# A hybrid attention and state-space block on one core: table order, load queues and the pace of side work

## The chip, the cores and the metric

The kernel runs on one core of a Trainium2 chip. The metric is the device time of one execution in microseconds, as the median of several; the profile is of one execution.

## The reference

One layer of a streaming encoder, for 2048 new frames (the prompt) and 64 next frames of a running stream with 2048 cached frames (the sample). Cut to what matters here:

```
h = rms(x);  q, k, v, fg, u, hc, gb, gc = split(h @ w_in)       # 8 heads of 64; 16 state-space groups
c = cumsum(log_sigmoid(fg))
att = softmax(q k^T / 8 + c_q - c_k, causal) v                  # prompt: 2048 x 2048 per head
                                                                # sample: 64 x (2048 cached + 64)
h_t = A h_(t-1) + B u_t;  y = Re(C h_t) + d u                   # state space ("s5"), complex diagonal A
ssm = gelu(y) * sigmoid(gelu(y) @ w_glu + b_glu)
conv = gb * (three taps over gc * hc)
x = x + concat[rms(att), rms(ssm), rms(conv)] @ w_out
x = x + relu(rms(x) @ w_up)^2 @ w_down
```

All of it is float32, and the outputs are also the keys, values, gates and last states.

## The kernel before

The program has these stages: the projection (0 to 542.6 us in the profile), attention (542.6 to 1185.5), the output projection, the up and the down projection. Only the attention stage is touched.

**Products.** A float32 value is split into a high part `ph` (rounded to the format fp32r, for which TensorE has a quick product) and a low part `pl`, the difference. The probabilities times the values are three products: `ph` with both parts of `v` (L1260, L1262) and `pl` with the high one (L1267). Plain float32 products are used in the side work.

**Attention of the prompt.** Heads go one after the other. A head has four query blocks of 512 (`sb`), and for each the key tiles of 128 in pairs; that gives 24 units in a fixed list (`order()`). A unit does the scores of its tiles (two products, L1239 and L1240, `st`), the exponential on ScalarE (`p`, L1248), its rounding on ScalarE (`ph`, L1251) and the low part (`pl`, L1252) on VectorE or GpSimd. The products with `v` follow some units later (`pend`, `pend2`). Beside this, the row maxima of the next head are found: products `mx` (L1149) and VectorE's reductions `pm` (L1154). The tiles of a head are `kb`, `q1`, `ka` (2 MB together, loaded by `load(h + 1)` at a head's first unit), `v3`, and `q2` by query block (`load_q2`, three buffers), all loaded on SP's queue.

**Side work.** A chain of generators runs between the units. `s5_branch` makes tables on GpSimd and VectorE (`tables(q)`, four times: `z` and `e`, each a sum of two outer products with temporaries `tz` and `te`), then transposes and products on PE (`s5pg`, `s5pk`, `s5ps`), writes a kernel `kp_d` to memory, and loads it back in 8 shifted copies of 256 KB as a Toeplitz matrix (`s5mt`, L922). Then comes the recurrence over 16 steps of rows on GpSimd (L931 to L935), and the attention of the sample (`sample_attention`, for the pairs of heads 0 and 1, then 2 and 3); at last the outputs `s5py`, the gated unit `s5pz` (L1020), the loads of `w_out` and `out_sample`.

**What sets the order.** `fill(w)` is called in each unit with the unit's weight `w` (2.2 for a pair of full tiles, 1.2 on the diagonal; 40.8 in a head). It moves a clock on by 1.68 `w` and adds `w` to a budget (at most 4). While the budget is positive and the clock has come to the time that the chain asked for, the chain takes its next step; a step that yields a number above 0 costs 0.4 and is not gone on with before that much clock has passed, one that yields 0 costs 1.25. So each engine's list of instructions is fixed when the program is built; nothing is decided on the chip.

```
def fill(w):
    clock.now += w * 1.68
    clock.budget = min(clock.budget + w, 4.0)
    while clock.budget > 0 and clock.now >= clock.ready:
        y = next(it, None)
        ...
        clock.ready = max(clock.now + y, clock.ready)
        clock.budget -= 0.4 if y > 0 else 1.25
```

Of the kernel before, what the change touches and what calls it, by code (L numbers as in the profile page):

```python
# [13 lines left out]
ALU = mybir.AluOpType  # L14
# [34 lines left out]
def f32(ap):  # L49
    return ap.bitcast(F32)  # L50
# [735 lines left out]
def s5_branch(g, pool, sp):  # L786

    nc, I, O = g.nc, g.I, g.O
# [62 lines left out]
    po.memset(kp[:, :, 0:112], 0.0)  # L851

    def tables(q):
        z = zts[q % 2]
        gs = slice(4 * q, 4 * q + 4)
        sh = [128, 4, 16, 16]
        tz = tt[:, :1024].rearrange("p (g s c) -> p g s c", g=4, s=16)
        for dst, a, b in ((z, u1, bbr), (tz, u2, bbi)):
            g.tc.keep_in_program_order(po.tensor_tensor(
                dst, a.rearrange("p s g -> p g s")[:, gs].unsqueeze(3).to_broadcast(sh),  # L860
                b[:, gs].unsqueeze(2).to_broadcast(sh), op=ALU.mult))
        po.tensor_tensor(z, z, tz, op=ALU.add)
        sh = [128, 4, 17, 16]
        te = te_t.rearrange("p (g s c) -> p g s c", g=4, s=17)
        for eng, dst, a, b in ((ve, e_t[:, gs], v1, ctr), (po, te, v2, cti)):
            g.tc.keep_in_program_order(eng.tensor_tensor(
                dst, a.rearrange("p s g -> p g s")[:, gs].unsqueeze(3).to_broadcast(sh),
                b[:, gs].unsqueeze(2).to_broadcast(sh), op=ALU.mult))
            yield 2
        g.tc.keep_in_program_order(ve.tensor_tensor(e_t[:, gs], e_t[:, gs], te, op=ALU.add))  # L870
        yield 2

    yield from tables(0)
# [1 line left out]
    for q in range(4):  # L875
# [3 lines left out]
        z = zts[q % 2]  # L879
# [41 lines left out]
    for t in range(8):
        nc.sync.dma_start(mt[16 * t:16 * t + 16],  # L922
                          g.kp_d[:, :, 16 * (7 - t):16 * (7 - t) + 256].rearrange("g c n -> c g n"))
        yield 1
# [243 lines left out]
def attention(ctx, g, fill):  # L1168

    tc, nc = g.tc, g.nc  # L1170
# [25 lines left out]
    def load(h):  # L1196
        i, hp, e = h % 2, h // 2, h % 2
        r = slice(64 * e, 64 * e + 64)
        qk = g.qk_d[hp]
        nc.sync.dma_start(f32(kb[i])[64:67, :], g.nc_d[:, h, :])  # L1200
        nc.sync.dma_start(f32(kb[i])[0:64, :], qk[0, 1, r, :])
        nc.sync.dma_start(f32(q1[i])[0:64, :], qk[0, 0, r, :])
        nc.sync.dma_start(f32(ka[i])[0:64, :], qk[0, 1, r, :])
        nc.sync.dma_start(f32(ka[i])[64:128, :], qk[1, 1, r, :])
        if h == 0:
            load_q2(0, 3)
            nc.scalar.dma_start(f32(q1[i])[64:67, :], g.m_d)
            load_v(0)
# [20 lines left out]
    def scores(h, sb, batch, first, last):  # L1229
# [19 lines left out]
            parts.append((kt, c0, p, ph, pl))  # L1249
        for j, (kt, c0, p, ph, pl) in enumerate(parts):  # L1250
            nc.scalar.activation(ph[:, c0:], p[:, c0:], AF.Copy)  # L1251
            (nc.gpsimd if g.idle and j else nc.vector).tensor_tensor(pl[:, c0:], p[:, c0:], f32(ph)[:, c0:],  # L1252
                                                                     op=ALU.subtract)

        def high():
# [41 lines left out]

    units = order()
    total = sum(u[4] for u in units)
    fill(0.1)  # L1300
    load(0)
    pend, pend2 = [], []

    def late(n, m):
# [8 lines left out]
    for h in range(H):  # L1313
        mx = max_items(h + 1) if h + 1 < H else iter(())
        owed = 0.0

        def maxima():
            nonlocal owed
            if owed >= 1:
                next(mx, None)  # L1320
                owed -= 1

        for n, (sb, batch, first, last, w) in enumerate(units):
            if n == 0 and h + 1 < H:
# [12 lines left out]
            if n >= 2:  # L1337
                owed += 43.0 * w / (total * 0.74)
            maxima()
            if len(pend) > 2:  # L1340
                f, f2 = pend.pop(0)
                f()
                pend2.append(f2)
            maxima()
            fill(w)
            if len(pend2) > 1:
                pend2.pop(0)()
            maxima()
# [507 lines left out]
def hybrid_step_kernel(ctx, tc, I, O, dbg=None):  # L1856
# [3 lines left out]
    with ExitStack() as c2:  # L1860
# [31 lines left out]
        def side_by_side(*gens):  # L1892
            ready = {x: clock.now for x in gens}
            while ready:
                x = min(ready, key=ready.get)
                if ready[x] > clock.now:
                    yield ready[x] - clock.now
                y = next(x, None)
                if y is None:
                    del ready[x]  # L1900
                else:
                    ready[x] = clock.now + y
                    if y == 0:
                        yield 0
# [63 lines left out]
```

## Time and profile before

| | |
|---|---|
| median of 3 runs | 2793.95 us (2791.91 to 2795.13) |
| profiled execution | 2794.95 us, of which the span is 2793.2 |
| mean granted TensorE clock | 0.979 |
| PE busy | 2699.9 us (97%) |
| DVE, ACT, POOL busy | 1681.7, 1230.3, 415.4 us |
| attention stage | 542.6 to 1185.5 us: 642.9 us |

The span is what the profiler saw from the first instruction to the last; what lies around it belongs to the time of the execution. PE is TensorE, DVE is VectorE, ACT is ScalarE, POOL is GpSimd, SP the engine that here only issues transfers. Matmuls are pipelined and their ends are modelled, so a busy PE can still be one at half clock; the granted clock (PEclk, as a share of 2.4 GHz) and the number of products in a stretch tell the two apart.

### The profile page before, as it was taken

The page shows a single profiled execution, that of the slowest core. Times are in us where ns is not written, and L with a number is a line of the kernel's source. Part 1 is how long each engine was busy: PE and PEld are TensorE (multiplying, and loading weights), DVE is VectorE, ACT ScalarE, POOL GpSimd, SP SyncE. Part 2 cuts the span into 40 slices and gives each one's busy share as a digit, 9 for nine tenths or more (in the row PEclk, how much of TensorE's full clock was granted, in tenths as well). Part 3 has the DMA queues.
Part 4 walks back from the last instruction along what each step waited for, and adds up shares of the span by engine and source line. Part 5 has one row for each costly group of instructions (what it writes and reads, how often), then busy time and mean ns, then how long its engine had stood idle before and what let it go on. Part 6 is the DMA issues. An engine that isn't in the chain of part 4 may idle for free.

```text
span 2793.2 us, 38960 instructions
## 1 busy us (share of the span) xinstructions
PE 2699.9 (97%) x14438; PEld 2341.8 (84%) x14438; DVE 1681.7 (60%) x3375; ACT 1230.3 (44%) x2383; POOL 415.4 (15%) x566
## 2 busy tenths in 40 slices
PE   7999999888899999899989999999999999999999
PEld 7999998755567776688789999999998888888887
DVE  7637468477575576577786686686644344434433
ACT  5424243156577677833265676576641111111110
POOL 2101105123752224432300000000000000000000
PEclk9999999989899999999999999999999999999999
DMA  7636546643644223375545353344354122212123
GB/s 216 186 109 185 165 104 177 111 99 93 108 100 109 72 71 89 116 213 165 177 137 176 131 176 127 133 156 136 128 198 151 51 78 80 78 48 78 49 79 117
DMA packets 358929, 347.13 MB, mean 124 GB/s; under 512 B 43726, under 2 KB 316446, under 8 KB 354734
## 3 DMA queue, kind: packets, MB, share of 16 engines
q1 hardware_dynamic: 356189, 336.87, 41.8%
q0 software_dynamic: 2240, 7.01, 0.8%
q8 instruction: 114, 1.87, 0.3%
q14 instruction: 76, 0.62, 0.1%
q10 hardware_dynamic: 310, 0.75, 0.1%
HBM read 237.05 MB, written 107.46 MB: 123 GB/s over the span
## 4 chain that ended last, share of the span: by engine, by line
PE 85%; DMA 4%; issue 4%; DVE 3%; ACT 2%; POOL 1%; SPq 1%; ACTq 0%; DVEq 0%; POOLq 0%
PE pa L1641 12%; PE pd L107 8%; PE pd L108 8%; PE pd L106 8%; PE pd L1641 6%; PE pb L1641 3%; PE pq L106 3%; PE pq L108 3%; PE pq L107 3%; PE mx L1149 2%; PE po L106 2%; PE st L1239 2%; PE po L107 2%; PE po L108 2%; PE st L1240 2%
## 5 line engine op out<-in xcount | busy, mean ns | idle before, releaser
L1820 DVE TENSOR_TENSOR acc<-acc,pd 128x512 f32<-128x512 f32 x272 | 186.7, 686 | 411.2 <-PE pd L108 406.0
L106 PE MATMUL pd<-dw,fh 128*128 128x512 f32 x1016 | 395.2, 389 | 0.0
L108 PE MATMUL pd<-dw,fl 128*128 128x512 f32 x1016 | 395.2, 389 | 0.0
L107 PE MATMUL pd<-dw,fh 128*128 128x512 f32 x1016 | 395.2, 389 | 0.0
L1789 ACT ACTIVATE fh<-fr 128x512 fp32r<-128x512 f32 x127 | 80.2, 632 | 530.9 <-PE pd L107 520.9
L1252 DVE TENSOR_TENSOR pl<-p,ph 128x512 fp32r<-128x512 f32 (+2 forms) x246 | 171.5, 715 | 110.7 <-ACT ph L1251 104.5
L107 PEld LDWEIGHTS pd<-dw,fh 128*128 128x128 f32 x1016 | 190.7, 188 | 39.7
L108 PEld LDWEIGHTS pd<-dw,fl 128*128 128x128 f32 x1016 | 190.7, 188 | 39.6
L106 PEld LDWEIGHTS pd<-dw,fh 128*128 128x128 f32 x1016 | 190.7, 188 | 39.5
L1154 DVE TENSOR_REDUCE pm<-mx 128x1 f32<-128x512 f32 (+2 forms) x320 | 184.3, 607 | 58.7 <-PE mx L1153 32.3
L1248 ACT ACTIVATE p<-st 128x512 f32<-128x512 f32 (+2 forms) x320 | 164.3, 544 | 89.8 <-PE st L1240 34.2
L1641 PE MATMUL pa<-as,wt 128*128 128x352 f32 x1152 | 201.3, 323 | 0.8 <-ACT sm L1656 0.8
L1641 PEld LDWEIGHTS pa<-as,wt 128*128 128x128 f32 x1152 | 187.3, 188 | 2.0 <-ACT sm L1656 1.3
L106 PE MATMUL pq<-wh,xh 128*128 128x384 f32 (+1 forms) x512 | 179.4, 350 | 5.2 <-ACT xh L233 4.7
L1251 ACT ACTIVATE ph<-p 128x512 fp32r<-128x512 f32 (+2 forms) x320 | 173.8, 581 | 3.9 <-PE po L1262 1.8
L108 PE MATMUL pq<-wh,xl 128*128 128x384 f32 (+1 forms) x512 | 174.5, 341 | 0.5 <-DVE xl L234 0.3
L107 PE MATMUL pq<-wl,xh 128*128 128x384 f32 (+1 forms) x512 | 174.1, 340 | 0.0
L1586 DVE TENSOR_TENSOR wt<-tt,wt 128x512 fp32r<-128x512 f32 x192 | 131.4, 687 | 69.1 <-ACT wt L1585 65.9
L1586 DVE TENSOR_TENSOR w<-wr,w 128x512 fp32r<-128x512 f32 x144 | 99.0, 688 | 87.2 <-ACT w L1585 86.9
L1585 ACT ACTIVATE wt<-tt 128x512 fp32r<-128x512 f32 x192 | 120.4, 627 | 67.2 <-PE pd L1641 66.2
L1240 PE MATMUL st<-q,ka 128*128 128x512 f32 (+2 forms) x320 | 124.4, 393 | 12.0 <-DMA q<-qk_d 12.0
L1149 PE MATMUL mx<-kb,q 66*128 66x512 f32 (+2 forms) x280 | 113.4, 438 | 18.1 <-DVE pm L1154 11.1
(508 smaller groups left out, 6118.6 us busy)
## 6 DMA issues: line engine op xcount, KB each, us to landing
wr<-in_w_up_dram SPq DMA_DIRECT2D x46, 1024.0 KB
f_d<-sm SPq DMA_DIRECT2D x47, 704.0 KB
fr<-f_d SPq DMA_DIRECT2D x128, 256.0 KB
raw<-in_w_in_dram SPq DMA_DIRECT2D x51, 512.0 KB
dr<-in_w_down_dram SPq DMA_DIRECT2D x32, 512.0 KB
qk_d<-stgT SPq DMA_DIRECT2D x16, 768.0 KB
xt<-in_x_prompt_dram SPq DMA_DIRECT2D x16, 512.0 KB
ka<-qk_d SPq DMA_DIRECT2D x16, 512.0 KB
```

What stands on the lines that cost most here:

```text
L106: nc.tensor.matmul(out, lh, rh, start=first, stop=False)
L107: nc.tensor.matmul(out, lh, rl, start=False, stop=False)
L108: nc.tensor.matmul(out, ll, rh, start=False, stop=last)
L1149: nc.tensor.matmul(p[:, :n], q1[0:66, t * 128:t * 128 + 128], kb[0:66, k0 * 128:k0 * 128 + n], start=True, stop=not last)
L1154: nc.vector.tensor_reduce(pm[:, t, c:c + 1], p[:, :n], axis=AX.X, op=ALU.max)
L1240: nc.tensor.matmul(st[:, c0:], ka[i][:, kc], q2[h, sb][:, c0:512], start=False, stop=r < 0)
L1248: nc.scalar.activation(p[:, c0:], st[:, c0:], AF.Exp)
L1251: nc.scalar.activation(ph[:, c0:], p[:, c0:], AF.Copy)
L1252: (nc.gpsimd if g.idle and j else nc.vector).tensor_tensor(pl[:, c0:], p[:, c0:], f32(ph)[:, c0:], op=ALU.subtract)
L1586: ve.tensor_tensor(t[:, 1], x, f32(t)[:, 0], op=ALU.subtract)):
L1641: nc.tensor.matmul(bank, w[:, x, k], a[:, y, k], start=first and k + j == 0, stop=k + j == 5, skip_group_check=not first)
L1820: nc.vector.tensor_tensor(a[:, o], a[:, o], p, op=ALU.add)
```

## The change

Five edits, all in the attention stage: the order of the instructions inside `tables(q)` and its yields; the loads of the Toeplitz copies, from SP's queue inside `s5_branch` to ACT's queue beside the second part of the sample attention, at least 4 units of the clock apart; `load(0)` ahead of the first `fill`, and `ka` loaded in one transfer of 128 partitions instead of two of 64; `fill(0.5 * w)` twice in a unit instead of `fill(w)` once; and GpSimd takes the second low part of a pair from the clock's time at the recurrence plus 80 on, instead of after sample pairs 0 and 1.

```
@@ -851,23 +851,29 @@
     po.memset(kp[:, :, 0:112], 0.0)
 
     def tables(q):
+        gs = slice(4 * q, 4 * q + 4)
         z = zts[q % 2]
-        gs = slice(4 * q, 4 * q + 4)
-        sh = [128, 4, 16, 16]
         tz = tt[:, :1024].rearrange("p (g s c) -> p g s c", g=4, s=16)
-        for dst, a, b in ((z, u1, bbr), (tz, u2, bbi)):
-            g.tc.keep_in_program_order(po.tensor_tensor(
-                dst, a.rearrange("p s g -> p g s")[:, gs].unsqueeze(3).to_broadcast(sh),
-                b[:, gs].unsqueeze(2).to_broadcast(sh), op=ALU.mult))
-        po.tensor_tensor(z, z, tz, op=ALU.add)
-        sh = [128, 4, 17, 16]
         te = te_t.rearrange("p (g s c) -> p g s c", g=4, s=17)
-        for eng, dst, a, b in ((ve, e_t[:, gs], v1, ctr), (po, te, v2, cti)):
+
+        def outer(eng, dst, a, b):
+            sh = [128, 4, dst.shape[2], 16]
             g.tc.keep_in_program_order(eng.tensor_tensor(
                 dst, a.rearrange("p s g -> p g s")[:, gs].unsqueeze(3).to_broadcast(sh),
                 b[:, gs].unsqueeze(2).to_broadcast(sh), op=ALU.mult))
-            yield 2
-        g.tc.keep_in_program_order(ve.tensor_tensor(e_t[:, gs], e_t[:, gs], te, op=ALU.add))
+
+        def add(eng, dst, x):
+            g.tc.keep_in_program_order(eng.tensor_tensor(dst, dst, x, op=ALU.add))
+
+        outer(po, te, v2, cti)
+        yield 2
+        outer(po, z, u1, bbr)
+        outer(ve, e_t[:, gs], v1, ctr)
+        yield 3
+        outer(po, tz, u2, bbi)
+        add(ve, e_t[:, gs], te)
+        yield 3
+        add(po, z, tz)
         yield 2
 
     yield from tables(0)
@@ -918,10 +924,14 @@
         nc.sync.dma_start(hs[hh, 129, :], I[src][0, 0].rearrange("g p -> p g"))
 
     mt = pool.tile([128, G, 256], F32, tag="gm", name="s5mt")
-    for t in range(8):
-        nc.sync.dma_start(mt[16 * t:16 * t + 16],
-                          g.kp_d[:, :, 16 * (7 - t):16 * (7 - t) + 256].rearrange("g c n -> c g n"))
-        yield 1
+
+    def toeplitz():
+        for t in range(8):
+            yield 4
+            ac.dma_start(mt[16 * t:16 * t + 16],
+                         g.kp_d[:, :, 16 * (7 - t):16 * (7 - t) + 256].rearrange("g c n -> c g n"))
+
+    g.toeplitz = toeplitz
     r1 = sp.tile([128, 16, G], F32, tag="yg", bufs=3, name="s5r1")
     r2 = sp.tile([128, 16, G], F32, tag="yg", bufs=3, name="s5r2")
 
@@ -1200,8 +1210,7 @@
         nc.sync.dma_start(f32(kb[i])[64:67, :], g.nc_d[:, h, :])
         nc.sync.dma_start(f32(kb[i])[0:64, :], qk[0, 1, r, :])
         nc.sync.dma_start(f32(q1[i])[0:64, :], qk[0, 0, r, :])
-        nc.sync.dma_start(f32(ka[i])[0:64, :], qk[0, 1, r, :])
-        nc.sync.dma_start(f32(ka[i])[64:128, :], qk[1, 1, r, :])
+        nc.sync.dma_start(f32(ka[i]), qk[:, 1, r, :])
         if h == 0:
             load_q2(0, 3)
             nc.scalar.dma_start(f32(q1[i])[64:67, :], g.m_d)
@@ -1249,7 +1258,7 @@
             parts.append((kt, c0, p, ph, pl))
         for j, (kt, c0, p, ph, pl) in enumerate(parts):
             nc.scalar.activation(ph[:, c0:], p[:, c0:], AF.Copy)
-            (nc.gpsimd if g.idle and j else nc.vector).tensor_tensor(pl[:, c0:], p[:, c0:], f32(ph)[:, c0:],
+            (nc.gpsimd if g.clock.now > g.idle and j else nc.vector).tensor_tensor(pl[:, c0:], p[:, c0:], f32(ph)[:, c0:],
                                                                      op=ALU.subtract)
 
         def high():
@@ -1297,8 +1306,8 @@
 
     units = order()
     total = sum(u[4] for u in units)
+    load(0)
     fill(0.1)
-    load(0)
     pend, pend2 = [], []
 
     def late(n, m):
@@ -1337,12 +1346,13 @@
             if n >= 2:
                 owed += 43.0 * w / (total * 0.74)
             maxima()
+            fill(0.5 * w)
             if len(pend) > 2:
                 f, f2 = pend.pop(0)
                 f()
                 pend2.append(f2)
             maxima()
-            fill(w)
+            fill(0.5 * w)
             if len(pend2) > 1:
                 pend2.pop(0)()
             maxima()
@@ -1864,9 +1874,9 @@
         def chain():
             for y in s5_branch(g, fpool, fsp):
                 if y < 0:
+                    g.idle = clock.now + 80
                     yield from sample_attention(g, fpool, fsp, (0, 1))
-                    g.idle = True
-                    yield from sample_attention(g, fpool, fsp, (2, 3))
+                    yield from side_by_side(sample_attention(g, fpool, fsp, (2, 3)), g.toeplitz())
                 else:
                     yield y
 
@@ -1918,7 +1928,7 @@
 
         g.ah = c2.enter_context(tc.tile_pool(name="ah", bufs=1, reuse_waits="tile"))
         g.os = c2.enter_context(tc.tile_pool(name="os", bufs=2, reuse_waits="tile"))
-        g.ready, g.prep, g.late, g.idle = {}, {}, False, False
+        g.ready, g.prep, g.late, g.idle, g.clock = {}, {}, False, math.inf, clock
         g.fpool, g.fsp = fpool, fsp
         with ExitStack() as c2a:
             attention(c2a, g, fill)
```

The order on GpSimd (POOL), first tables, in head 0. `s5te` and `s5zt` are the temporaries and the first `z`, `s5zk` the second `z`; the `e` half stands on VectorE. `s5bg` is a bias of the gated unit. Before:

```order
L859 TENSOR_TENSOR s5zt_7016<-s5sc_6583 128x1024 x2
L961 TENSOR_SCALAR s5bg_10805<-s5bg_10805 128x2
L862 TENSOR_TENSOR s5zt_7016<-s5zt_7016 128x1024
L866 TENSOR_TENSOR s5te_6582<-s5sc_6583 128x1088
L859 TENSOR_TENSOR s5zk_7019<-s5sc_6583 128x1024
L859 TENSOR_TENSOR s5zt_7016<-s5sc_6583 128x1024
L862 TENSOR_TENSOR s5zk_7019<-s5zk_7019,s5zt_7016 128x1024
L866 TENSOR_TENSOR s5te_6582<-s5sc_6583 128x1088
```

After:

```order
L861 TENSOR_TENSOR s5te_6591<-s5sc_6592 128x1088
L861 TENSOR_TENSOR s5zt_6976<-s5sc_6592 128x1024 x2
L971 TENSOR_SCALAR s5bg_10084<-s5bg_10084 128x2
L866 TENSOR_TENSOR s5zt_6976<-s5zt_6976 128x1024
L861 TENSOR_TENSOR s5te_6591<-s5sc_6592 128x1088
L861 TENSOR_TENSOR s5zk_6979<-s5sc_6592 128x1024
L861 TENSOR_TENSOR s5zt_6976<-s5sc_6592 128x1024
L866 TENSOR_TENSOR s5zk_6979<-s5zk_6979,s5zt_6976 128x1024
```

The product into `s5te` stood behind the three of `z` and now stands first; the sum into `z` (L866 after) comes last.

The order on SP (transfers) from the end of head 1 into head 2. `s5mt` are Toeplitz copies, `kb1`, `q11`, `ka1` the tiles of the next head, `q22_0` the `q2` tile of head 2, block 0, `sa_y0` and `sa_c01` tiles of the sample attention, `mt2` a row of maxima on its way into `q10`, `s5hs` the starting state of the recurrence. Before:

```order
L922 DMA s5mt_8061<-kp_d_70 16x16x256 x2
L1164 DMA q10_6571<-mt2_8117 1x16x128
L922 DMA s5mt_8061<-kp_d_70 16x16x256 x4
L1200 DMA kb1_6577<-nc_d_80 3x2048
L1201 DMA kb1_6577<-qk_d1_61 64x2048
L1202 DMA q11_6578<-qk_d1_61 64x2048
L1203 DMA ka1_6575<-qk_d1_61 64x2048
L1204 DMA ka1_6575<-qk_d1_61 64x2048
L922 DMA s5mt_8061<-kp_d_70 16x16x256
L1220 DMA q22_0_8243<-qk_d1_61 64x512
L1221 DMA q22_0_8243<-qk_d1_61 64x512
```

After:

```order
L924 DMA s5hs_7978<-in_state_ssm_re_dram 64x16x1
L924 DMA s5hs_7978<-in_state_ssm_im_dram 64x16x1
L1094 DMA sa_y0_8335<-in_cache_k_dram 128x4x128
L1229 DMA q22_0_8447<-qk_d1_61 64x512
L1230 DMA q22_0_8447<-qk_d1_61 64x512
L1210 DMA kb1_6577<-nc_d_80 3x2048
L1211 DMA kb1_6577<-qk_d1_61 64x2048
L1212 DMA q11_6578<-qk_d1_61 64x2048
L1213 DMA ka1_6575<-qk_d1_61 128x1x2048
L1087 DMA sa_c01_8427<-ncs_d_82 4x1x512
L1094 DMA sa_y0_8335<-in_cache_k_dram 128x4x128
```

The Toeplitz copies are gone from this queue, and `q22_0` stands ahead of the next head's tiles instead of behind them.

The order on PE in head 6, from the scores of block 2 with key tile 8 on (`st6_2_8`). `s5pz` is a side product. Before:

```order
L1239 MATMUL st6_2_8_12505<-q10_6571,kb0_6570 128x512
L1240 MATMUL st6_2_8_12505<-q26_2_12199,ka0_6572 128x512
L1149 MATMUL mx7_12_1_12460<-kb1_6577,q11_6578 128x512
L1244 LDWEIGHTS identb_93
L1244 MATMUL st6_2_8_12505<-maskk_100,identb_93 128x128
L1260 MATMUL po6_2_12518<-ph6_2_0_12408,v30_6573 65x512
L1149 MATMUL mx7_12_2_12467<-kb1_6577,q11_6578 128x384
L1262 MATMUL po6_2_12518<-ph6_2_0_12408,v30_6573 64x512
L1260 MATMUL po6_2_12518<-ph6_2_1_12415,v30_6573 65x512
L1262 MATMUL po6_2_12518<-ph6_2_1_12415,v30_6573 64x512
L1020 MATMUL s5pz00_12471<-s5gt0_11129,s5wg_10803 128x266
L1020 MATMUL s5pz00_12471<-s5gt1_11936,s5wg_10803 128x266
```

After:

```order
L1248 MATMUL st6_2_8_12691<-q10_6571,kb0_6570 128x512
L1249 MATMUL st6_2_8_12691<-q26_2_12445,ka0_6572 128x512
L1253 LDWEIGHTS identb_93
L1253 MATMUL st6_2_8_12691<-maskk_100,identb_93 128x128
L1159 MATMUL mx7_13_0_12701<-kb1_6577,q11_6578 128x512
L1269 MATMUL po6_2_12704<-ph6_2_0_12623,v30_6573 65x512
L1271 MATMUL po6_2_12704<-ph6_2_0_12623,v30_6573 64x512
L1269 MATMUL po6_2_12704<-ph6_2_1_12630,v30_6573 65x512
L1271 MATMUL po6_2_12704<-ph6_2_1_12630,v30_6573 64x512
L1159 MATMUL mx7_13_1_12709<-kb1_6577,q11_6578 128x512
```

The products `s5pz` stood here and are now in head 5; only attention's own products and the maxima of head 7 (`mx7`) are left.

## Rows read from the trace of the kernel before

**Rows 1.** Windows, one row for each head; length, busy PE, PEld, DVE, ACT, POOL (count), clock, DMA, GB/s.

```profile
542.60:637.80 95.20, 74.00 (x339) 49.05 (x338) 62.98 (x103) 47.91 (x103) 25.97 (x15) 0.78 0.47 94
637.80:722.10 84.30, 76.62 (x388) 51.78 (x387) 58.49 (x100) 52.34 (x105) 26.73 (x32) 0.92 0.45 91
722.10:806.90 84.80, 77.01 (x363) 50.55 (x362) 56.75 (x92) 51.26 (x104) 76.75 (x146) 0.90 0.52 101
806.90:885.00 78.10, 77.72 (x424) 54.09 (x423) 48.75 (x90) 56.39 (x115) 12.41 (x12) 1.00 0.41 102
885.00:966.90 81.90, 81.75 (x447) 59.39 (x447) 46.95 (x96) 52.74 (x108) 18.77 (x16) 1.00 0.35 86
966.90:1041.90 75.00, 74.23 (x428) 56.72 (x428) 52.03 (x114) 53.84 (x121) 18.00 (x15) 1.00 0.28 71
1041.90:1119.70 77.80, 75.77 (x354) 53.75 (x353) 52.90 (x87) 59.94 (x128) 36.35 (x46) 0.91 0.39 106
1119.70:1185.50 65.80, 57.83 (x275) 39.87 (x275) 36.67 (x60) 58.94 (x112) 30.69 (x25) 0.96 0.37 112
2100.00:2200.00 100.00, 100.00 (x443) 82.81 (x442) 40.98 (x60) 15.62 (x23) 0.00 (x0) 1.00 0.36 109
```

**Rows 2.** Groups of instructions by line, 540 to 1190 us: busy, mean ns, idle before.

```profile
L1240 PE MATMUL st<-q,ka 128*128 128x512 f32 x224 | 93.3, 421 | 12.0 <-DMA q<-qk_d 12.0
...
L1090 PE MATMUL sa_ps<-sa_y,qbd 128*128 128x512 f32 x32 | 17.9, 641 | 0.0
```

**Rows 3.** Windows of four short stretches: tables twice, head 2's stall, a side-free stretch.

```profile
602.50:624.60 22.10, 14.63 (x47) 8.67 (x46) 18.48 (x21) 6.97 (x12) 16.37 (x8) 0.67 0.00 0
644.60:653.50 8.90, 5.40 (x15) 3.06 (x15) 5.33 (x8) 4.42 (x9) 2.46 (x2) 0.67 1.00 210
...
729.70:748.60 18.90, 11.53 (x35) 6.30 (x33) 6.90 (x12) 2.35 (x5) 17.51 (x24) 0.67 0.99 154
1153.80:1173.60 19.80, 19.80 (x98) 13.70 (x98) 9.92 (x15) 19.27 (x40) 9.39 (x8) 1.00 0.32 84
```

**Rows 4.** Timeline of POOL (start, us, instruction, idle before): tables, recurrence, low parts.

```profile
598.46 5.08 POOL L859 TENSOR_TENSOR s5zt<-s5sc 128x1024 f32<-128x1024 f32 x2
...
606.51 2.12 POOL L866 TENSOR_TENSOR s5te<-s5sc 128x1088 f32<-128x1088 f32 x1
...
712.58 0.22 POOL L931 TENSOR_TENSOR s5r<-s5aw,s5hs 64x16 f32<-64x16 f32 x1 [37.38 <-ACT p L1248]
...
807.33 0.77 POOL L935 TENSOR_TENSOR s5hs<-s5r,s5r 128x240 f32<-128x240 f32 x1
...
833.72 2.17 POOL L1252 TENSOR_TENSOR pl<-p,ph 128x512 fp32r<-128x512 f32 x2 [25.62 <-ACT ph L1251]
```

**Rows 5.** Timeline of DVE while the first tables are made.

```profile
603.36 0.73 DVE L1252 TENSOR_TENSOR pl<-p,ph 128x512 fp32r<-128x512 f32 x1
...
608.67 3.09 DVE L870 TENSOR_TENSOR s5e<-s5e,s5te 128x1088 f32<-128x1088 f32 x1 [3.51 <-POOL s5te L866]
...
612.02 2.17 DVE L1252 TENSOR_TENSOR pl<-p,ph 128x512 fp32r<-128x512 f32 x1
...
614.11 1.28 DVE L1154 TENSOR_REDUCE pm<-mx 128x1 f32<-128x512 f32 x2
...
631.19 1.28 DVE L870 TENSOR_TENSOR s5e<-s5e,s5te 128x1088 f32<-128x1088 f32 x1
```

**Rows 6.** Timeline of PE: the first score product, and one beside the tables.

```profile
555.07 1.19 PE L1240 MATMUL st<-q,ka 128*128 128x512 f32 x2 [11.61 <-DMA q<-qk_d]
...
612.15 0.80 PE L1149 MATMUL mx<-kb,q 66*128 66x512 f32 x1 [5.35 <-DVE pm L1154]
```

**Rows 7.** Waits, 540 to 1190 us: us in total, times, longest us.

```profile
DVE s5e L870 <- POOL s5te L866: 7.9, 2, 4.4
```

**Rows 8.** Chain of waits from 714 to 730 us: start, us, what.

```profile
716.49 1.86 SPq L922
...
727.60 19.29 DMA q<-qk_d
```

More of the change, by code (lines that the diff above doesn't have):

```diff
@@ L853, in tables, with outer @@
     def tables(q):
+        gs = slice(4 * q, 4 * q + 4)
         z = zts[q % 2]
-        gs = slice(4 * q, 4 * q + 4)
-        sh = [128, 4, 16, 16]
         tz = tt[:, :1024].rearrange("p (g s c) -> p g s c", g=4, s=16)
[L858 to L863, printed above, removed]
         te = te_t.rearrange("p (g s c) -> p g s c", g=4, s=17)
-        for eng, dst, a, b in ((ve, e_t[:, gs], v1, ctr), (po, te, v2, cti)):
+        def outer(eng, dst, a, b):
+            sh = [128, 4, dst.shape[2], 16]
             g.tc.keep_in_program_order(eng.tensor_tensor(
@@ L868, in tables, with add @@
                 b[:, gs].unsqueeze(2).to_broadcast(sh), op=ALU.mult))
-            yield 2
-        g.tc.keep_in_program_order(ve.tensor_tensor(e_t[:, gs], e_t[:, gs], te, op=ALU.add))
+        def add(eng, dst, x):
+            g.tc.keep_in_program_order(eng.tensor_tensor(dst, dst, x, op=ALU.add))
+        outer(po, te, v2, cti)
+        yield 2
+        outer(po, z, u1, bbr)
+        outer(ve, e_t[:, gs], v1, ctr)
+        yield 3
+        outer(po, tz, u2, bbi)
+        add(ve, e_t[:, gs], te)
+        yield 3
+        add(po, z, tz)
         yield 2
@@ L920, in s5_branch, with toeplitz @@
     mt = pool.tile([128, G, 256], F32, tag="gm", name="s5mt")
[L921 to L924, printed above, removed]
+    def toeplitz():
+        for t in range(8):
+            yield 4
+            ac.dma_start(mt[16 * t:16 * t + 16],
+                         g.kp_d[:, :, 16 * (7 - t):16 * (7 - t) + 256].rearrange("g c n -> c g n"))
+    g.toeplitz = toeplitz
     r1 = sp.tile([128, 16, G], F32, tag="yg", bufs=3, name="s5r1")
@@ L1202, in load @@
         nc.sync.dma_start(f32(q1[i])[0:64, :], qk[0, 0, r, :])
-        nc.sync.dma_start(f32(ka[i])[0:64, :], qk[0, 1, r, :])
-        nc.sync.dma_start(f32(ka[i])[64:128, :], qk[1, 1, r, :])
+        nc.sync.dma_start(f32(ka[i]), qk[:, 1, r, :])
         if h == 0:
@@ L1251, in scores @@
             nc.scalar.activation(ph[:, c0:], p[:, c0:], AF.Copy)
-            (nc.gpsimd if g.idle and j else nc.vector).tensor_tensor(pl[:, c0:], p[:, c0:], f32(ph)[:, c0:],
+            (nc.gpsimd if g.clock.now > g.idle and j else nc.vector).tensor_tensor(pl[:, c0:], p[:, c0:], f32(ph)[:, c0:],
                                                                      op=ALU.subtract)
@@ L1299, in attention @@
     total = sum(u[4] for u in units)
+    load(0)
     fill(0.1)
-    load(0)
     pend, pend2 = [], []
@@ L1339, in attention @@
             maxima()
+            fill(0.5 * w)
             if len(pend) > 2:
@@ L1344, in attention @@
             maxima()
-            fill(w)
+            fill(0.5 * w)
             if len(pend2) > 1:
@@ L1866, in chain @@
                 if y < 0:
+                    g.idle = clock.now + 80
                     yield from sample_attention(g, fpool, fsp, (0, 1))
-                    g.idle = True
-                    yield from sample_attention(g, fpool, fsp, (2, 3))
+                    yield from side_by_side(sample_attention(g, fpool, fsp, (2, 3)), g.toeplitz())
                 else:
@@ L1920, in hybrid_step_kernel @@
         g.os = c2.enter_context(tc.tile_pool(name="os", bufs=2, reuse_waits="tile"))
-        g.ready, g.prep, g.late, g.idle = {}, {}, False, False
+        g.ready, g.prep, g.late, g.idle, g.clock = {}, {}, False, math.inf, clock
         g.fpool, g.fsp = fpool, fsp
```

## The prediction

> **What bounds the kernel now.** I read the table of windows first, cut at the times at which the first product of each attention head starts [rows 1]. The edit touches nothing outside these eight heads, so everything from 0 to 542.6 us and from 1185.5 us on stays at its price. In the table compare PE's busy time with the length of the head, and both with the last row, a stretch of another stage in which PE never stops: 443 products of 512 columns in 100 us, 0.226 us each. Heads 3 to 6 are nearly full; heads 0 to 2 hold 95.2, 84.3 and 84.8 us with PE busy 74.0 to 77.0, at a granted clock of 0.78, 0.92 and 0.90 of 2.4 GHz; head 7 has 57.8 of 65.8.
>
> Busy time flatters a slow clock, so I used a second measure: the PE work that stands in each head. Counting the products in the order of the two programs, in columns/512, times 0.226 us, gives PE's content. A plain f32 product counts as four: the profile lists each as two instructions, 641 ns where an fp32r one has 421 [rows 2], so a pitch of about 0.45 us each, an estimate from these two rows. Contents of before, heads 0 to 7: 55.9, 65.2, 63.6, 70.4, 72.2, 66.0, 65.6, 49.7, sum 508.6. Of after: 55.9, 63.8, 77.6, 82.9, 65.3, 73.0, 47.6, 42.4, sum 508.5. Nothing is saved on PE; side work moves from heads 6 and 7 into heads 2 and 3. Content by length is 0.877 over the undisturbed heads 3 to 6 (274.2 of 312.8 us), 0.77 in head 1.
>
> The third and fourth views, waits and chain, say what makes heads 0 to 2 poor. VectorE's `s5e` addition waits for GpSimd's `s5te` twice, 7.9 us in all [rows 7], and PE stands behind the maxima queued after it, 5.35 us once [rows 6]. In head 2 the chain of waits goes through a `q2` tile: 19.29 us of DMA [rows 8], and that stretch of 18.9 us holds 35 products [rows 3].
>
> **The change part by part.**
>
> *Tables.* Same instructions, another order: `te` is now GpSimd's first, and VectorE gets its addition one step later. The table stretch of head 0 takes 22.1 us for 47 products, that of head 1 8.9 us for 15 [rows 3]; at 0.226 us and the ratio 0.877 these would be 12.1 and 3.9, so 10 and 5 us are lost. What goes is the wait: `te` ends 10.2 us after the first table instruction in before, and would end after 2.1 [rows 4]. What stays is VectorE's own slowness while GpSimd works: 2.17 us for a low part that takes 0.73 alone, 3.09 for an addition that takes 1.28 [rows 5]. Two or three such instructions per table, 1.4 to 1.8 us each, remain, partly beside PE work. I take −8 in head 0, and −6 in head 1 (its stretch and a little of the next table); bounds 0 and −15 together.
>
> The Trainium skill, "SBUF — State Buffer" (Who interferes with whom), says that a VectorE instruction with two SBUF inputs is blocked for the whole of a GpSimd instruction that reads SBUF, and that a reduction never is. The rows agree: the slowed ones are tensor_tensor, and two reductions behind the slowed low part take 0.64 us each [rows 5]. By that rule the reorder only shifts the blocking, and four additions and low parts at 1.4 to 1.8 us on the path would take 6 to 7 of the 14 us back.
>
> *Toeplitz loads.* Eight loads of 256 KB leave SP for ACT's queue and are spread over the head and a half after sample pairs 0 and 1, at least 4 units of planner time apart. In before they stand ahead of `kb1`, `q11`, `ka1` and `q22`, and `q22` takes 19.29 us. PE isn't idle all that time: its 35 products are worth 7.9 us, 9.0 at the ratio 0.877, so the stretch loses 10 us; had PE nothing else to do, it would lose nearly all of its 18.9 us. In the new order `q22` is issued before the next head's loads and with no `s5mt` ahead. The stall goes: −10, bounds 0 (another transfer takes its place) and −16. On ACT an issue costs up to 1.86 us [rows 8], eight at most 15 us over more than a head; ACT is idle 22 to 34 us in each of heads 2 and 3 [rows 1], so I take 0.
>
> *First loads.* `load(0)` goes ahead of a 720 KB side load, and `ka` comes in one transfer. The first score waits 11.61 us for `q2` [rows 6], which is loaded after `ka`; before and after the DMA engines hardly move until that time because of what ran earlier. I take 0, bounds −2 and +2.
>
> *Two offers per unit.* The same budget, spent in halves, so side work comes in smaller pieces and, with GpSimd's and VectorE's table work earlier, ends in head 5 instead of 7. This is worth only what heads 2 to 5 cost when they are fuller. At 0.877: 77.6 gives 88.5, 82.9 gives 94.5, 65.3 gives 74.5, 73.0 gives 83.2. Head 6 becomes free of side work: PE's content is 47.6, ACT's own work is about 47.9 (head 0, where the side work on ACT is small), and a side-free stretch of before has ACT busy 19.27 of 19.80 us [rows 3]; so 49 at least, and I take 52. Head 7 loses 7.2 us of content, 8.2 at 0.877: 57.6.
>
> *GpSimd's share.* Low parts go to GpSimd from 80 planner units after the recurrence is issued, 78 in all instead of 74. GpSimd's first low part is an x2 row of 2.17 us at 833.72 in before; the recurrence holds GpSimd from 712.58 to 807.33, 95 us [rows 4]. 80 units are 1.17 heads, about 90 to 100 us in the heads at issue, so the first low parts may stand behind the recurrence's end by 0 to 8 us, and PE's low products with them. I take 0 and put 8 in the range. VectorE is freed of four instructions of 0.73 us [rows 5], beside other work: 0.
>
> **Sum.** Heads 0 to 7: 95.2−8 = 87.2; 84.3−6 less 1.4/0.877 of content = 76.7; 88.5; 94.5; 74.5; 83.2; 52; 57.6. Together 614.2 against 642.9 (542.6 to 1185.5): −28.7. Head 2's stall is not a term beside these: its 88.5 holds it as gone. The profiled execution took 2794.95 us (span 2793.2 and 1.75 around it), so 2766.2; the median of the runs lies 1.0 below: 2765.
>
> **Rivals.**
>
> *Waits stay (smaller gain).* GpSimd's tables block VectorE as before and the low parts queue behind the recurrence: half of the 14 us of the tables is lost and about 5 are added, 2777. For it: the slowed instructions [rows 5]. Against: 5.35 us of PE's wait is behind one instruction that no longer waits.
>
> *`q2` tiles behind 2 MB of the next head (slower).* SP now runs ahead of PE less evenly; in the new order `q23` (head 3) stands behind `kb0`, `q10`, `ka0` of head 4 and cache loads of the sample attention, and heads 2 and 5 have similar places. If a `q2` is issued so late there that PE waits, each costs what the queue cost in head 2, 10 to 16 us. One makes 2775 to 2781, two 2785 to 2797, three 2795 to 2813; it decides at two of the dear kind or three of the cheap one. For it: the 18.9 us stretch. Against: in before the same tile order in heads 3 to 6 showed no such wait, and side loads are smaller than the 2 MB of `s5mt`.
>
> *Work only moves.* Heads 2 to 5 fall to head 1's ratio: 298.8/0.773 = 386.5 instead of 340.7, +45.8, 2811; halfway there is no change. For it: head 2 keeps the recurrence on GpSimd, 76.75 of 84.8 us busy [rows 1], next to more PE work. Against: head 2 without its 10 us would be 63.6/74.8, a ratio of 0.85 with the same recurrence.
>
> **How the numbers follow.** The forecast 0.62 (own range 2752 to 2777), waits stay 0.18, late `q2` 0.11 (0.03 faster, 0.03 same, 0.05 slower), work only moves 0.09 (0.02, 0.02, 0.05). A measurement of this kernel tells from no change about 0.2%, 5.6 us. Of the first two cases 0.03 falls within that, 0.02 is left for slower by something unnamed: faster 0.80, same 0.08, slower 0.12. Low end: heads 2 to 5 at head 3's ratio of before (70.4/78.1, 0.90) give 332 instead of 341, −9; head 6 at ACT's 49, −3; the tables at −15, −1; first loads −2; head 7 at 54, −4: 2746. High end: one late `q2` and the smaller gain of the tables, 2792.
>
> **What the new profile would show.** Right: no `s5e` wait for `s5te` over 1 us; head 2 near 88 us with no stretch under a third full; head 3 the longest of heads 2 to 6; head 6 near 52 with ACT busy over 0.9. Wrong: PE waiting over 5 us for a `q2` transfer in heads 2, 3 or 5; low products waiting for GpSimd at the recurrence's end; heads 2 and 3 together above 200 us. A head 6 that stays above 60 would falsify the gain from the side work's earlier end.

## The result, and the profile after

The changed kernel takes 2934.67 us (median of 4, 2930.15 to 2936.74) against 2792.93 for the kernel before: a ratio of 1.0504, 95% interval 1.0486 to 1.0523. The forecast was 2765. The whole difference lies in the attention stage: 784.3 us in the profile, where it was 642.9. The windows by head, cut as in [rows 1] (length, busy time of PE, PEld, DVE, ACT, POOL, granted clock, DMA share, GB/s):

```profile
543.50:670.20 126.70, 81.33 (x337) 53.07 (x338) 66.54 (x91) 48.57 (x103) 28.65 (x14) 0.70 0.31 72
670.20:763.70 93.50, 76.50 (x376) 52.23 (x376) 56.73 (x101) 50.62 (x100) 12.40 (x10) 0.84 0.29 71
763.70:891.60 127.90, 94.93 (x460) 62.72 (x459) 59.02 (x105) 59.82 (x124) 77.08 (x166) 0.83 0.39 86
891.60:1016.20 124.60, 99.26 (x533) 71.50 (x532) 51.04 (x110) 60.38 (x125) 15.16 (x13) 0.88 0.28 67
1016.20:1105.70 89.50, 75.32 (x426) 55.99 (x425) 57.19 (x120) 57.33 (x133) 19.86 (x16) 0.92 0.28 76
1105.70:1203.10 97.40, 81.02 (x387) 57.20 (x386) 61.55 (x103) 64.76 (x129) 41.59 (x52) 0.93 0.35 100
1203.10:1274.50 71.40, 53.23 (x261) 36.25 (x260) 37.38 (x67) 41.55 (x84) 18.23 (x15) 0.88 0.27 71
1274.50:1327.80 53.30, 50.12 (x245) 34.90 (x245) 24.05 (x34) 48.79 (x97) 26.10 (x20) 0.97 0.33 94
```

Read the length, the clock and the DMA share together. Heads 0, 2 and 3 last 124 to 128 us; the clock is below full in every head, and the DMA share is lower than before in heads 0 to 4 (0.28 to 0.39, where [rows 1] has 0.35 to 0.52), though the same bytes are moved. The DMA engines are less busy and PE waits for them. PE's longest waits in total (us, times, longest):

```profile
PE st L1249 <- DMA q<-qk_d: 68.3, 4, 22.6
PE po L1269 <- ACT ot L1280: 44.3, 4, 16.0
PE sa_ps L1101 <- DMA sa_c<-ncs_d: 25.2, 3, 23.8
```

Only the first of the three is for `q2` tiles: outputs (`ot` waits for its buffer, and that for the write to `mix_d`) and side loads (`sa_c`) are late too. So I looked at one stall closely, at the start of head 5. What SP issues there:

```profile
1102.62 0.50 SPq L1229 DMA_DIRECT2D q<-qk_d  x1
1104.05 0.26 SPq L1210 DMA_DIRECT2D kb<-nc_d  x1
1104.36 0.46 SPq L1211 DMA_DIRECT2D kb<-qk_d  x1
1104.87 0.59 SPq L1212 DMA_DIRECT2D q<-qk_d  x1
1105.56 0.55 SPq L1213 DMA_DIRECT2D ka<-qk_d  x1
1106.15 0.48 SPq L1230 DMA_DIRECT2D q<-qk_d  x1
```

`q2` comes in two halves. The first stands ahead of the next head's loads, the second right behind `ka`, which is now one transfer. The chain of waits there, start, us, what:

```profile
1106.15 29.01 DMA q<-qk_d
1135.16 0.04 issue
1135.20 0.79 PE st L1249
```

A half of a `q2` tile, 128 KB (64 rows of 512 f32), takes 29 us, and PE stands still for the last 12.5 of them. Where the time goes is seen in the DMA's share and rate in the 40 slices of 1 us from 1100 to 1140 us:

```profile
DMA  0000393989761111169799881111111111111600
GB/s 0 8 0 12 127 131 123 270 172 246 145 131 51 49 57 57 49 164 172 221 172 229 156 229 41 49 49 49 49 49 57 57 45 55 41 41 33 150 8 0
```

A digit of 1 is a tenth to a fifth of the 16 DMA engines; with it go 33 to 57 GB/s, for 18 us in all: about 0.9 MB, most of the 1 MB of `ka`. In the kernel before, the same loads (two transfers for `ka`) at the start of head 5, 964 to 1004 us, look so:

```profile
DMA  0999999999968699200000634000053001600060
GB/s 25 147 262 188 205 221 197 205 205 221 221 148 141 213 328 311 82 0 8 0 16 0 131 92 172 0 0 0 0 156 107 0 8 47 211 12 0 0 133 0
```

Mostly nines, at about 200 GB/s, and then only short bursts. In head 0 of the changed kernel there are 7 us in which no engine computes (window, columns as above):

```profile
590.00:597.00 7.00, 0.00 (x0) 0.00 (x0) 0.00 (x0) 0.00 (x0) 0.00 (x0) 0.50 0.12 51
```

0.12 of 16 is 1.9. So the merged transfer runs on about two of the sixteen engines, and what is behind it and has a part on those engines waits for it.

The trace also keeps the signals by which the parts of a transfer report that they have landed, and they show both. Each of the two `ka` loads of the kernel before gives 16 signals; the merged one gives one about 1 us after its issue and then only two, here at 1133.36 and 1134.84. The `q2` half issued at 1106.15 has 14 of its 16 by 1112.81 and the last two at 1133.67 and 1135.16, right behind those of `ka`; `v`, issued at 1117.09, has 14 by 1125.65 and the last two at 1137.43 and 1138.86. From its issue to its last signal the merged `ka` takes 26.7 to 38.9 us in the eight heads; in the kernel before the two loads at the start of head 5 take 8.8 and 10.2.

### The profile page after: what moved, and what is told of

Read it like the earlier page. It is cut to its first block, busy times and chain, and to the rows that moved or that the text cites. A ratio compares the mean times of both kernels' runs of the same rounds, so it can differ in the third digit from the quotient of the medians.

```text
span 2934.9 us, 38943 instructions
## 1 busy us (share of the span) xinstructions
PE 2716.8 (93%) x14438; PEld 2350.3 (80%) x14438; DVE 1684.3 (57%) x3371; ACT 1228.9 (42%) x2383; POOL 409.8 (14%) x570
## 4 chain that ended last, share of the span: by engine, by line
PE 79%; DMA 10%; DVE 6%; ACT 2%; issue 2%; SPq 1%; POOL 0%; ACTq 0%; DVEq 0%; POOLq 0%
PE pa L1651 12%; PE pd L107 8%; PE pd L108 8%; PE pd L106 8%; PE pd L1651 6%; PE pb L1651 3%; DMA mix_d<-ot 3%; PE pq L108 2%; PE pq L106 2%; PE pq L107 2%; DMA q<-qk_d 2%; PE mx L1159 2%; DMA sa_c<-ncs_d 2%; PE po L106 2%; PE po L107 2%
## 5 line engine op out<-in xcount | busy, mean ns | idle before, releaser
L106 PEld LDWEIGHTS pd<-dw,fh 128*128 128x128 f32 x1016 | 190.7, 188 | 39.6
L1269 PE MATMUL po<-ph,v 128*65 128x512 f32 (+2 forms) x320 | 130.2, 410 | 45.3 <-ACT ot L1280 44.3
```

The source lines that it names most:

```text
L106: nc.tensor.matmul(out, lh, rh, start=first, stop=False)
L1269: nc.tensor.matmul(acc[0:65, c0:512], v3[i][:, kt, 64:129], ph[:, c0:], start=first and j == 0, stop=False)
```

## The experiments

**The merged load undone.** Changed kernel, one line:

```
-        nc.sync.dma_start(f32(ka[i]), qk[:, 1, r, :])
+        nc.sync.dma_start(f32(ka[i])[0:64, :], qk[0, 1, r, :])
+        nc.sync.dma_start(f32(ka[i])[64:128, :], qk[1, 1, r, :])
```

> The changed kernel with one line undone: ka loaded in two transfers of 64 partitions again. Theory K (the merged ka load): its access pattern has an outermost count of 2, and it moves at 47 to 59 GB/s with a DMA share of 0.1 to 0.2 over some 20 us in each head, where the same bytes in two transfers moved at 200 GB/s and more; what SP issues behind it (q2 tiles, outputs, side loads) waits. Then this kernel takes about 2765 us (2746 to 2792), 140 to 190 less than the changed one. Rival S (SP's order and the fuller heads 2 and 3: q2 tiles late behind 2 MB whatever its form): 2890 or more.

Measured: 2793.72 us, ratio to before 1.000 (0.999 to 1.001). Theory K's mechanism holds, S falls: 141 us go away with this line. But K's number, 2765, is missed: the rest of the change is worth nothing, not 29 us. By head:

```profile
542.10:640.70 98.60, 76.58 (x339) 49.94 (x339) 66.79 (x101) 48.30 (x103) 32.61 (x18) 0.81 0.52 96
640.70:716.30 75.60, 72.25 (x377) 49.42 (x377) 56.50 (x101) 50.60 (x100) 12.75 (x8) 0.96 0.39 88
716.30:818.30 102.00, 90.68 (x459) 59.87 (x457) 62.28 (x104) 59.91 (x124) 83.47 (x167) 0.95 0.56 111
818.30:919.00 100.70, 97.40 (x532) 70.89 (x533) 52.03 (x112) 60.99 (x126) 15.04 (x13) 0.98 0.31 80
919.00:992.30 73.30, 72.80 (x424) 55.14 (x424) 56.53 (x120) 57.10 (x133) 19.08 (x16) 1.00 0.35 95
992.30:1075.10 82.80, 78.80 (x388) 56.05 (x387) 61.18 (x103) 64.36 (x129) 42.24 (x52) 1.00 0.42 118
1075.10:1132.80 57.70, 55.56 (x261) 37.77 (x260) 37.36 (x67) 41.82 (x84) 18.15 (x15) 0.91 0.36 87
1132.80:1184.60 51.80, 47.79 (x238) 33.13 (x237) 23.54 (x34) 48.79 (x97) 27.11 (x20) 0.95 0.31 88
```

**The merged load alone**, in the kernel before (the reverse edit):

> The kernel before with the merged ka load alone. Theory K: seven or eight heads lose 10 to 30 us each where something urgent stands behind ka on SP: 2870 to 2960. Rival S: ka is not needed until the next head, so the slow transfer is hidden: 2794, within 10.

Measured: 2910.2 us, 1.0416 (1.0400 to 1.0431), +116. K again. PE's longest wait in total, times, longest:

```profile
PE st L1239 <- DMA q<-qk_d: 63.1, 4, 19.0
```

**Cut by columns instead of by partitions.**

```
-        nc.sync.dma_start(f32(ka[i]), qk[:, 1, r, :])
+        nc.sync.dma_start(f32(ka[i])[:, 0:1024], qk[:, 1, r, 0:1024])
+        nc.sync.dma_start(f32(ka[i])[:, 1024:2048], qk[:, 1, r, 1024:2048])
```

> The changed kernel with ka in two transfers, cut by columns instead of by partitions, so each still has an outermost count of 2 and 128 partitions. Theory K (the shape decides): about as slow as the changed kernel, 2900 to 2950. Rival L (one transfer of 1 MB is too long, two of 512 KB are not): 2765, as with the cut by partitions.

Measured: 2926.47 us, 1.0476 (1.0456 to 1.0495). Two transfers of 512 KB each, as in the fast version, but with the 2 outermost: still slow. The length isn't it, the shape is. DMA share and rate at the same place (1094 to 1134 us) show the tenths twice:

```profile
DMA  0000129999921111111861198999611111111160
GB/s 0 8 0 0 20 78 246 225 180 188 156 49 57 53 49 53 53 49 57 209 193 29 41 164 246 229 188 213 131 45 53 37 57 49 49 51 49 33 148 10
```

**The merged load on ACT's queue**, in the changed kernel (`nc.scalar` for `nc.sync`).

> The changed kernel with the merged ka transfer issued from ACT instead of SP. Theory Q (the slow transfer hurts by what stands behind it on SP's queue): only head 0, which needs ka at once, stays 20 to 30 us too long, the rest is as with ka split: 2810 to 2830. Theory E (the two DMA engines that carry it are taken, whatever the queue): as slow as the changed kernel, 2900 or more.

Measured: 2895.83 us, 1.0366 (1.0351 to 1.0381). Both missed by their numbers, E by little: leaving SP's queue gives back 39 of 141 us, the other 102 stay. E's mechanism is in the trace: a `sa_y` load issued on SP's queue at 757.46, while `ka` is under way on ACT's (753.61 to 790.13), has 14 of its 16 signals by 761.57 and the last two at 779.41 and 781.36, and PE waits 9.17 us for it. But there is something else that neither theory had. The chain goes from `ka` to SP:

```profile
753.61 36.52 DMA ka<-qk_d
790.13 0.02 issue
790.15 0.58 SPq L1221
```

A transfer on SP's queue that is given the completion semaphore of `ka` in its turn waits until `ka` has landed, once for each of the eight loads of `ka`, 167.2 us together. SP's waits in total, times, longest:

```profile
SPq L1221 <- DMA ka<-qk_d: 73.6, 4, 27.6
SPq L1281 <- DMA ka<-qk_d: 65.4, 3, 25.3
SPq L1212 <- DMA ka<-qk_d: 28.2, 1, 28.2
```

So this run doesn't free SP's queue of `ka`. How the 102 us divide between this wait, the two shared engines and the lateness of `ka` itself (the first score of head 0 starts at 562.5 us, 20.4 later than with `ka` split) wasn't separated.

**The other parts, each alone in the kernel before.** Their diffs are the pieces of the change; only the parts named were put in.

> The kernel before with the reordered tables alone. Theory G (the forecast's terms hold one by one): 14 us less than before, 2780. Theory W (VectorE's two-input instructions stay slow while GpSimd makes the tables, whatever the order, and PE's work costs the same wherever it stands): within 4 us of before; head 0 keeps 20 us or so of PE idle time, against 21.2 in the kernel before.

> The kernel before with the Toeplitz loads moved to ACT's queue alone. Theory G: 10 us less, 2784. Theory W: PE is idle 7.8 us in head 2 of the kernel before, and its attention products take 57.9 us there instead of 55.4 at full clock; at most 6 to 10 us to be won, and another transfer may take the place: 0 to 10 us less.

> The kernel before with the two half offers of side work in a unit alone. Side work ends in head 5 here too. Theory G (the forecast's ratio 0.877 of content to length wherever side work stands): 10 us or more less than before, 2784. Theory W (heads 3 to 6 of before have 0.2 to 2 us of PE idle time each, so there is no gap for side work to fill): within 5 us of before.

> The kernel before with GpSimd's share of the low parts by the clock alone. Both theories: within 3 us of before; a third one (low parts queue behind the recurrence on GpSimd) 3 to 10 us more, with PE waiting for GpSimd's low parts in head 3.

| alone in the kernel before | us | ratio, 95% interval | forecast |
|---|---|---|---|
| tables | 2779.54 | 0.9943 (0.9931 to 0.9955) | −14 us |
| Toeplitz loads on ACT | 2796.04 | 1.0003 (0.9992 to 1.0015) | −10 us |
| two half offers | 2803.70 | 1.0031 (1.0019 to 1.0043) | about −5 (what is left of the sum) |
| GpSimd's share by the clock | 2795.36 | 0.9996 (0.9987 to 1.0004) | 0 |
| merged `ka` | 2910.20 | 1.0416 (1.0400 to 1.0431) | 0, at most 2 |

The tables agree with G, the Toeplitz loads with W, the share with both, and the half offers with neither: they cost 8.7 us (1.0031 of 2795). In the trace of the Toeplitz version head 2 is longer, 106.5 us for 84.8, and heads 3 to 7 are together some 16 us shorter; PE waits in head 2 in total, times, longest:

```profile
PE sa_ps L1095 <- DMA sa_c<-ncs_d: 8.7, 1, 8.7
PE mx L1153 <- DMA q<-qk_d: 6.0, 1, 6.0
PE sa_pk L1085 <- DMA sa_y<-in_cache_k_dram: 4.3, 1, 4.3
```

In the kernel before the stop in head 2 was not a wait for `q2`, whose 19.29 us of [rows 8] cost PE 0.43. It stood before the first product of the maxima of head 3, which needs that head's `q1` tile:

```profile
738.83 0.55 PE L1149 MATMUL mx<-kb,q 66*128 66x256 f32 x1 [6.26 <-issue]
```

The last signal of that `q1` load comes at 738.74. With the Toeplitz copies on ACT's queue the same product waits 6.0 us for its `q1`, which lands at 745.59, and the sample attention waits for its own loads besides.

**load(0) behind the first offer again**, with `ka` split.

```
-    load(0)
     fill(0.1)
+    load(0)
```

> The changed kernel with ka in two transfers and load(0) behind the first offer of side work again, so the first loads stand wholly as before. Theory K: within 3 us of the version that only splits ka. Rival F (the 720 KB side load ahead of load(0) matters by itself): 5 to 15 us slower than that version.

Measured: 2790.97 us, 0.9989 (0.9975 to 1.0003), beside 1.000 (0.999 to 1.001) with `load(0)` first: K, not F. The intervals overlap: at most some us. With `load(0)` first the stage waits for `v` in place of `q2` (PE, total, times, longest; [rows 6] had 11.61 us):

```profile
PE po L1270 <- DMA v<-v_d: 10.0, 1, 10.0
```

**Is it the tables' order or their pace?** In the change a call of `tables` also asks for 10 units of the planner's clock instead of 6. New order, old pace:

```
         outer(po, z, u1, bbr)
         outer(ve, e_t[:, gs], v1, ctr)
-        yield 3
+        yield 2
         outer(po, tz, u2, bbi)
         add(ve, e_t[:, gs], te)
-        yield 3
         add(po, z, tz)
         yield 2
```

> The kernel before with the tables' instructions in the new order, but the same three steps and the same planner time in a call of tables as before (2, 2, 2), so all later side work stands where it stood. Theory O (the order: te first, VectorE's addition no longer waits): as good as the reordered tables with their longer pace, about 2780. Theory P (the pace: tables take 10 units of planner time instead of 6 in a call, and the later side work comes later, away from the congested heads 1 and 2): within 4 us of before; between the two, both have a part.

Measured: 2793.68 us, 0.9998 (0.9988 to 1.0008): no gain, though two of its 12 runs (2781.41 and 2783.06) lie near the time of the reordered tables and the other ten between 2790 and 2799. The wait itself is gone; the trace has one the other way, GpSimd for VectorE, which none of PE's waits shows:

```profile
POOL s5te L861 <- DVE s5e L866: 11.3, 2, 10.1
```

(The profiled execution is the one of 2781.41 us, so its waits may not be those of the median.) Old order, new pace:

```
-            yield 2
+            yield 3
         g.tc.keep_in_program_order(ve.tensor_tensor(e_t[:, gs], e_t[:, gs], te, op=ALU.add))
-        yield 2
+        yield 4
```

> The kernel before with its own order in the tables, but the longer pace of the changed one: 10 units of planner time in a call (3, 3, 4) instead of 6. Theory P (the pace makes the gain): 2777 to 2784. Theory OP (order and pace are both needed): within 4 us of before, or half of the 16 us.

Measured: 2795.52 us, 0.9997 (0.9989 to 1.0006): no gain either, so OP. And the pace taken further, 4, 5, 5, 4 with the new order:

> The kernel before with the reordered tables and a still longer pace: 18 units in a call (4, 5, 5, 4) instead of 10. Theory P, taken further (side work is worth more the further it is spread from heads 1 and 2 over the later heads): 3 to 10 us less than the reordered tables, 2770 to 2777. Rival: the gain is used up once the tables' work no longer meets the heads' busy places, and side work is pushed behind the last head, where nothing covers it: 2780 to 2795.

Measured: 2801.57 us, 1.0018 (1.0009 to 1.0027): the rival, and beyond its upper end. What it named is in the trace: after the last head PE waits for side work that nothing covers.

```profile
PE pss L1436 <- POOL mr L1431: 15.3, 1, 15.3
```

So the 16 us appear only with both, at this pace. One difference is in the traces: with the old order and the new pace, PE waits for `q2` twice, 26.6 us in all, the longer 15.5 and in head 2; with the reordered tables 14.3, of which 11.4 at the stage's start. Old order, new pace first (PE, total, times, longest):

```profile
PE st L1240 <- DMA q<-qk_d: 26.6, 2, 15.5
```

```profile
PE st L1246 <- DMA q<-qk_d: 14.3, 2, 11.4
```

Without the 15.5 us the old order at the new pace would stand at 2780, the time of the reordered tables: an estimate, and no run tests it. The kernel before waits for `q2` no longer than the reordered tables do (12.0 us), so this is not what they gain against it; that shows in the windows of heads 0 to 2 and 7 of the reordered tables alone:

```profile
542.20:635.00 92.80, 75.35 (x339) 48.40 (x339) 64.29 (x100) 47.73 (x103) 25.23 (x15) 0.80 0.52 103
635.00:706.90 71.90, 66.38 (x345) 44.57 (x345) 62.14 (x104) 50.98 (x99) 17.39 (x9) 0.98 0.33 81
706.90:780.60 73.70, 68.85 (x335) 45.50 (x334) 52.10 (x87) 48.57 (x95) 52.94 (x117) 0.95 0.65 104
1089.70:1171.90 82.20, 74.50 (x341) 53.81 (x341) 40.13 (x63) 67.35 (x130) 50.20 (x54) 0.94 0.36 115
```

Against [rows 1] head 1 is 12.4 us shorter and head 2 11.1, both at a higher clock (0.98 and 0.95, where they had 0.92 and 0.90), while head 7 is 16.4 longer with the side work that moved there.

**Combinations**, in search of a better version: tables with the share; and tables, Toeplitz loads and share (the changed kernel without the half offers and without the first loads' edits).

> The kernel before with the reordered tables and GpSimd's share by the clock. Both theories: within 3 us of the reordered tables alone, 2777 to 2783.

> The changed kernel without the two half offers and without the first loads' edits: tables, Toeplitz loads and share. Theory W: the Toeplitz move gains nothing by itself, as measured, so about 2780. Theory G: its 10 us were hidden by another stall that the tables' later pace removes, so 2770 to 2775.

Measured: 2783.33 us, 0.9958 (0.9945 to 0.9971), and 2785.75 us, 0.9969 (0.9958 to 0.9980). The first lies at the upper end of what was expected of it, the second 6 us above the nearer theory, W. Both are faster than before; neither beats the tables alone, which has the lowest time of the versions run here (its interval and that of tables with share overlap), 0.57% under the kernel before and 5.3% under the changed one.

## Why the prediction was wrong

**The step that failed is "First loads".** It put `ka` "in one transfer" at 0, with bounds −2 and +2, arguing from what the DMA engines do before the first score. The load is in every head, and its price came from the transfer's shape, which I never looked at: the order shows `128x1x2048` on the side of the tile, but the source is two blocks of 64 rows. It costs 141 us in the changed kernel and 116 in the kernel before. The Trainium skill, "DMA: Bandwidth & Descriptors" (Why a DMA increments its semaphore by 16 and not by 1), says that a transfer from SP or ACT is split over the largest number of engines up to 16 that divides the slowest dimension of both sides. For 2 and 128 that is 2 engines; the two late signals of each merged `ka`, and the share of 0.12 from 590 to 597 us, at 51 GB/s, agree with 2 of 16.

**The rival on late `q2` tiles** had the right symptom, a `q2` half behind the next head's loads, at 10 to 16 us a place and three places. It took this price from the queue in head 2; the trace has four waits of PE for `q2`, of 12.5 to 22.6 us, two in heads 3 and 5, which it named, and two in head 0, which it didn't, and waits for outputs and side loads too. With `ka` split the order of SP's queue that it feared is the same and those stalls are gone, so its mechanism isn't what made the kernel slow.

**The rest, tested with `ka` split: forecast −29 us, measured 0.** By head, forecast against measured: 87.2 and 98.6; 76.7 and 75.6; 88.5 and 102.0; 94.5 and 100.7; 74.5 and 73.3; 83.2 and 82.8; 52 and 57.7; 57.6 and 51.8. Heads 0 and 2 hold 25 of the missing 28 us.

- *The ratio 0.877* stood for a gap that side work could fill. I split PE's time by the starts and ends of its products in the trace, into attention's products, side products and time with none in flight:

| | attention | side | none | sum |
|---|---|---|---|---|
| before | 472.0 | 123.0 | 48.0 | 642.9 |
| `ka` split | 469.9 | 122.1 | 50.6 | 642.7 |
| tables alone | 467.3 | 122.7 | 39.6 | 629.6 |
| changed kernel | 483.9 | 127.7 | 172.6 | 784.2 |

Before has 0.2 to 2.0 us of "none" in each of heads 3 to 6. Their products stand further apart than 0.226 us per 512 columns: attention's own content of a head, 49.4 us when counted as in the prediction, takes 55 to 56 in heads 3 to 5, at full clock. (A product is listed for about 0.4 us and can be followed after 0.23, so waits of under 0.2 us between products don't show as "none".) By this split, moving side work there and back moves its cost along; only the 48 us, and the slow products of heads 0 to 2, 6 and 7, could be won. The rival "work only moves" was nearer to the truth than the forecast: what it gave for half of its way, no change, is what was measured, and its whole way, 2811 with head 1's poor ratio, was too much.

- *Tables*: −14 forecast, −16 measured alone, but not for the reason given, so that the numbers agree is luck: with the wait gone and nothing else changed the median doesn't move. VectorE's slowness stays; in the version with `ka` split, VectorE's rows beside GpSimd's tables:

```profile
604.93 2.83 DVE L861 TENSOR_TENSOR s5e<-s5sc 128x1088 f32<-128x1088 f32 x1
...
608.88 1.91 DVE L866 TENSOR_TENSOR s5e<-s5e,s5te 128x1088 f32<-128x1088 f32 x1
...
614.87 3.86 DVE L1262 TENSOR_TENSOR pl<-p,ph 128x512 fp32r<-128x512 f32 x2
...
636.08 4.35 DVE L1262 TENSOR_TENSOR pl<-p,ph 128x256 fp32r<-128x256 f32 x2
```

An addition takes 1.91 and low parts 1.93 (512 columns) and 2.18 us each (x2 rows of 3.86 and 4.35), where [rows 5] has 1.28 and 0.73 (512 columns) undisturbed. The rule of the Trainium skill that the prediction weighed ("SBUF — State Buffer", Who interferes with whom) agrees. In head 0 PE waits 7.1 us for VectorE's low parts and maxima with `ka` split and 7.4 before, so the reorder left these waits as they were. PE's time without a product in head 0 is 22.0 us, after 21.2 before; the rest of it is mostly the wait for `v`, 10.0, where before it was `q2`, 11.6.

- *Toeplitz*: −10 forecast, 0 measured. The stop in head 2 was put down to `q2`, and it was a wait for the next head's `q1`, which stays; the bound "another transfer takes its place" was the case besides, with the sample attention's own loads. ACT's issues, put at up to 1.86 us from a row of SP, took 0.31 to 0.33.
- *Two half offers*: a few us gained, by the forecast; 8.7 lost. They pull side work into heads 1 to 3: in that version heads 1 to 3 take 298 us for 247 before, and heads 5 to 7 some 180 for 219.
- *Share*: 0 forecast, 0 measured. Low parts did not queue behind the recurrence in a way that shows.
- *What the new profile would show*: of the signs for right, head 6 near 52 (57.7 with `ka` split, with ACT busy 0.72, not over 0.9) failed even there. Of the signs for wrong, PE waiting over 5 us for a `q2` transfer and heads 2 and 3 above 200 us (252.5, and 202.7 with `ka` split) came true.

Left open: why the reordered tables gain only at their own pace, beyond the `q2` waits shown; and why 16 us become 9 when the Toeplitz loads and the share, each worth nothing alone, stand beside the tables (0.9969). The half offers then take these 9 away, as they cost 8.7 alone, and the sum is the 0 that was measured with `ka` split.

## What to carry to other kernels

When a change merges transfers, look at the outermost count of the merged pattern on both sides before its bytes: here a count of 2 made a 1 MB load take 27 to 39 us and held up what came behind. Before counting a gap as room for other work, check that it is time without a product and not the pitch of the products. And test a reordering apart from the pace that comes with it: each alone gave nothing here.

## What the runs showed of the hardware

- One transfer from memory to 128 partitions whose source is two blocks was carried by two DMA engines: after the first signal it gave only two, where loads of 64 partitions give 16, and where it went alone it moved at 51 GB/s at a DMA share of 0.12. Cut into the two blocks, it moved with the loads around it at about 200 GB/s. Cutting it by columns into two changed little (2926 for 2935 us, against 2794).
- Later transfers passed it on the other engines: 14 of the 16 parts of a `q2` half landed within 7 us, and the two on its engines 29 us after the issue.
- Issuing it on ACT's queue instead of SP's took back 39 of 141 us. The two engines are shared between the queues (a `sa_y` load on SP's queue had 14 of 16 parts after 4 us and the last after 24), and SP's queue waited 167.2 us for the completion semaphores that `ka` held, as the program gives them out in turn to both queues.
- The same order of a few instructions on GpSimd and VectorE was worth 16 us or nothing, by the pace of the side work around it.
